# The low halves of 32 retrieval weights made early and read back from DRAM, and four gates moved

## Chip, cores and metric

The kernel runs on one core of a Trainium2 chip. The metric is the device time of one execution in microseconds (us). The engines are TensorE (PE; its weight loads are shown as PEld), VectorE (DVE), ScalarE (ACT), GpSimd (POOL) and SyncE (SP), which here does nothing but issue DMA transfers. The five run their own instruction streams in order, and an instruction that waits holds up those behind it.

## The reference

Two transformer blocks on 512 positions of width 1024, all in fp32, batch 1. The change touches the first. It computes, cut to what matters:

```python
h = modulate(rmsnorm(x, norm1_g), sh1, sc1)
q, k, v, gu, gv, ga, gb = split(h @ w_in)
y_a = neighborhood_attention(q, k, v, k_c, v_c, na_rpb)
y_b = spatial_gating(gu, gv, gm_ln_g, gm_ws, gm_bs)
x = x + g1 * (sigmoid(ga) * (y_a @ w_proj_a) + sigmoid(gb) * (y_b @ w_proj_b)) @ w_out
h2 = modulate(rmsnorm(x, norm2_g), sh2, sc2)
# peer_ffn, for each position, 8 heads:
s_top, i_top = top_k(q . sub_keys, 16)          # two halves of 128 keys
best_s, best_pos = top_k(all 16 x 16 sums, 16)  # which 16 of 16384 experts
wgt = softmax(best_s) * gelu(expert_u[experts] . h2)
x = x + g2 * sum(wgt * expert_v[experts])
```

Three of four position blocks compute the hidden values of all 16384 experts as dense products (128 weight blocks `uT[i]` of 128 experts each) and pick from them; the fourth block gathers its experts' rows.

## The kernel before

**Weights.** A product in fp32 is made of three fp32r products, hi·hi, hi·lo and lo·hi (`mm3`, L859 to L862). For each 512 KB weight block `weight` (L849 on) issues a load from SP into a `raw` buffer, ACT writes the rounded copy `hi` (L854), and DVE writes the rest, `lo` = raw - hi (L856). There are four `raw`, three `hi` and three `lo` buffers. A `raw` buffer is free when its `lo` is done. The rows `adar` of the modulation weights, which DVE accumulates through this whole stretch, take the same four buffers.

**Stages of the first block, by the trace.** Up to about 120 us the inputs, the modulation and the products `gv` and `gu`. To 176 us the second branch: gates 0 to 3 (`gate`, a product of 24 matmuls on a `win` block and a sigmoid), then a loop over eight output blocks b (12 matmuls each on half a `wpb` block), which for b of 4 to 7 computes gate b before the product. From 176 us the query, key and value products and the heads' attention, to 382 us. Then the loop over eight `wpa` half-blocks (to 404 us), the `wout` blocks (to 450 us), the retrieval's queries with their top 16 (475 to 572 us), and the retrieval proper:

```python
work = Work(*[retrieve(n) for n in range(NT - 1, -1, -1)])
while work.parts:
    spilled(first)
    work.go(RH)
    if len(work.parts) < NT:
        gat.go(GH0)
    first += 1
```

`spilled(i)` is the dense product of one `uT` block with 384 positions (24 matmuls) and a gelu (L377). Between the products the four blocks' retrieval steps go, interleaved: POOL forms the 256 sums of a head (`cand`, L306), DVE takes their top 16 (L272 to L276), DVE compares and POOL multiplies the expert indices (`eq`, L321 and L323, on POOL two in a row for each block), DVE adds them up (L329); and, for the gathered block, POOL issues indirect DMAs of 1 MB (`rows`, L178) that DVE reduces (L172, L169). After 740 us the remaining `uT` blocks go on without `retrieve`. The order of instructions on each engine is set by a scheduler when the kernel is built.

Of the kernel before, what the change touches and what calls it, by code (L numbers as in the profile page):

```python
# [8 lines left out]
F32 = mybir.dt.float32  # L9
F32R = mybir.dt.float32r  # L10
# [3 lines left out]
AF = mybir.ActivationFunctionType  # L14
# [4 lines left out]
P = 128  # L19
# [111 lines left out]
HALVES = slice(0, S // 2), slice(S // 2, S)  # L131
DT = 3
AB, LA = 3, 1
NR, TC, IG = 32, 24, 8
RH, GH0, BH, GH1, GF, GO, VP = 2.4, 1.0, 2.3, 1.2, 3.4, 4, 999


def peer(ctx, tc, I, banks, mod, mid, x1, R, vec, gain, ident, weight, mm3, proj, proj_many, split, enter):

    nc = tc.nc  # L140
    T = DT * P
    with ExitStack() as c2:
# [82 lines left out]
        with ExitStack() as c3:  # L225
# [2 lines left out]
            hl = phh.tile([P, KB, S], F32R, name="hl2")  # L228
            h = (hh, hl)
            bank = banks(mm=(4, 5, 6), S=(2, 3), T=(7, 0), h=(4, 5), o=(0, 2, 7, 3, 1, 6))  # L230
            sources, queue = [I["wq"][hp] for hp in range(NHP)] + [I["uT"][i] for i in range(P)], []

            def fill(n=3):
                while len(queue) < n and sources:
                    queue.append(weight(sources.pop(0)))

            with tc.tile_pool(name="tn", bufs=1) as tn:
                s2 = tn.tile([P, KB], F32, name="s2")
# [578 lines left out]
def body(ctx, tc, I, out):  # L817
# [32 lines left out]
    def weight(src, pool=False):  # L850
# [5 lines left out]
        (nc.gpsimd if pool else nc.vector).tensor_sub(lo, raw, hi.bitcast(F32))  # L856
        return hi, lo

    def mm3(ps, w, x, first, last):  # L859
        nc.tensor.matmul(ps, w[0], x[0], start=first, stop=False)  # L860
        nc.tensor.matmul(ps, w[0], x[1], start=False, stop=False)  # L861
        nc.tensor.matmul(ps, w[1], x[0], start=False, stop=last)  # L862
# [64 lines left out]
    with ExitStack() as c1:  # L927
# [175 lines left out]
            gate(gbm[:, n, :], 28 + n)  # L1103
            next(later, None)
        for b in range(KB):
            if b >= NT:
                gate(gbm[:, b, :], 28 + b)
            if b % 2 == 0:
                wb = weight(I["wpb"][b // 2])
            b_ps = bank("S")  # L1110
            proj(b_ps, wb, (ybh[:, 0], ybh[:, 1]), 4, (b % 2) * 4)
            nc.vector.tensor_mul(gbm[:, b, :], gbm[:, b, :], b_ps)
            next(later, None)
        c1g.close()

        sga = pz.tile([P, KB, S], F32, tag="sga", name="sga")
# [80 lines left out]
        for b in range(4):  # L1197
# [3 lines left out]
            for qb in range(4):  # L1201
                bias = bp.tile([P, 2, 256], F32, tag="bias", name="bias", bufs=2)
                nc.sync.dma_start(bias, I["bias"][qb * 4 + b])
                nc.gpsimd.tensor_add(bias, bias, mask[:, qb, :].unsqueeze(1).broadcast_to([P, 2, 256]))
                q, g = slice(qb * P, (qb + 1) * P), WIN[qb] * 64
                for j in range(2):
                    i = qb * 2 + j
                    s_ps = bank("S")
                    nc.tensor.matmul(s_ps, qs[:, j, q], window(kk, j, g), start=True, stop=False)
                    nc.tensor.matmul(s_ps, qx[:, j, q], window(kk, j, g), start=False, stop=True)  # L1210
                    nc.vector.tensor_add(s_ps[:, 0:256], s_ps[:, 0:256], bias[:, j, :])
                    nm = bp.tile([P, 1], F32, tag="nm", name="nm")
                    nc.vector.tensor_reduce(nm, s_ps, AX.X, ALU.max, negate=True)
                    pr = bp.tile([P, S], F32, tag="pr", name="pr")
                    nc.scalar.activation(pr, s_ps, AF.Exp, bias=nm, accum_out=rs[:, i:i + 1])
                    tp = bank("T")
                    for c in range(4):
                        nc.tensor.transpose(tp[:, c * P:(c + 1) * P], pr[:, c * P:(c + 1) * P], ident)
                    pT = bp.tile([P, 4, P], F32, tag="pT", name="pT")
                    if j:  # L1220
                        nc.scalar.activation(pT.rearrange("p j q -> p (j q)"), tp, AF.Copy)
                    else:
                        nc.vector.tensor_copy(pT.rearrange("p j q -> p (j q)"), tp)
                    for c in range(4):
                        v = VCH[qb][c] if c < 2 else 5 + c
                        nc.tensor.matmul(o_ps[:, i * 64:i * 64 + 64], pT[:, c, :], V9[:, v, j * 64:j * 64 + 64],
                                         start=c == 0, stop=c == 3)
                    if j and beside[b]:
                        beside[b].pop(0)()
                    next(later, None)  # L1230
            while beside[b]:
                beside[b].pop(0)()
# [18 lines left out]
        with tc.tile_pool(name="pm", bufs=1) as pm, tc.tile_pool(name="sr2", bufs=1) as sr:  # L1251
# [4 lines left out]
            for b in range(KB):  # L1256
# [4 lines left out]
                nc.vector.tensor_mul(sga[:, b, :], sga[:, b, :], a_ps)  # L1261
                nc.vector.tensor_add(sga[:, b, :], sga[:, b, :], gbm[:, b, :])
                split(mh[:, b, :], ml[:, b, :], sga[:, b, :])
            ms, held, R = bank("T"), {}, mid.tile([P, S], F32, name="nR")

            def wout(b, w, c=slice(0, S)):
# [9 lines left out]
            for b in range(KB):  # L1276
                late.append((b, weight(I["wout"][b])))
                if b < KB - 3:
                    wout(*late.pop())
            for half in HALVES:  # L1280
                for a in late:
                    wout(*a, half)
                rfactor(sr, ms[:, half], S // 2, into=R[:, half], tag="h")
    st = peer(ctx, tc, I, banks, mod, cm, x1, R, vec, gain, ident, weight, mm3, proj, proj_many, split, enter)
    second(ctx, tc, I, out, st, vec, gain, ident, ones, weight, mm3, proj, proj_many, squares, rsqrt, rfactor, split)


# [12 lines left out]
```

## Time and profile before

| | |
|---|---|
| median of 3 runs | 2567.55 us (2566.6 to 2568.09) |
| the profiled execution | 2567.01 us, its span 2565.2 us |
| mean granted clock | 0.987 |
| PE busy | 2487.4 us, 97% of the span |
| DVE, ACT, POOL busy | 70%, 42%, 12% |

The span is what the profiler records, from the first to the last instruction. Busy shares are averages over the whole span; the stages above have different limits.

### The profile page before, as it was taken

What the parts mean: (1) busy time and instruction counts of PE and PEld (TensorE: products, weight loads), DVE (VectorE), ACT (ScalarE), POOL (GpSimd) and SP (SyncE); (2) the same over time, 40 slices, a digit from 0 to 9 for tenths busy, and PEclk for the clock granted to TensorE, in tenths of its full rate; (3) what the DMA queues carried; (4) which work ended last, traced back from release to release, by engine and by line L of the source; (5) the groups of instructions that cost most, each with busy time, mean ns of one, the idle gap of its engine ahead of it and who ended that gap; (6) DMA issues with size and microseconds to landing.
All of it is one profiled execution on the core that took longest, in us unless ns stands there. A gap on an engine that the chain in (4) does not pass through costs nothing.

```text
span 2565.2 us, 34641 instructions
## 1 busy us (share of the span) xinstructions
PE 2487.4 (97%) x13153; PEld 2137.1 (83%) x13153; DVE 1795.4 (70%) x3041; ACT 1066.7 (42%) x1844; POOL 307.2 (12%) x198
## 2 busy tenths in 40 slices
PE   7999999998889999999999999998999999999998
PEld 4788888888889999999988888886788888888887
DVE  6656745899989888878888888877765334533345
ACT  6524453433344444444444433435433323422343
POOL 0001100004331111122222222200000000000000
PEclk8999999999899999999999999999999999999999
DMA  6353533325667888899998999972112233223254
GB/s 239 127 172 125 169 100 118 101 83 169 226 247 278 300 291 294 289 345 346 328 356 314 317 355 362 358 288 75 58 42 83 90 99 99 91 99 99 98 182 163
DMA packets 145814, 511.28 MB, mean 199 GB/s; under 512 B 13680, under 2 KB 39408, under 8 KB 125936
## 3 DMA queue, kind: packets, MB, share of 16 engines
q1 hardware_dynamic: 114464, 330.14, 37.7%
q0 software_dynamic: 18432, 134.23, 14.3%
q10 hardware_dynamic: 12752, 44.70, 4.6%
q8 instruction: 103, 1.69, 0.3%
q14 instruction: 63, 0.52, 0.1%
HBM read 465.50 MB, written 43.52 MB: 198 GB/s over the span
## 4 chain that ended last, share of the span: by engine, by line
PE 85%; DVE 10%; ACT 2%; issue 1%; DMA 1%; POOL 0%; DVEq 0%; SPq 0%; ACTq 0%; POOLq 0%
PE ps_mm L860 13%; PE ps_mm L862 13%; PE ps_mm L861 12%; PE ps_o L862 7%; PE ps_o L861 7%; PE ps_o L860 7%; PE ps_S L860 3%; PE ps_S L861 3%; PE ps_S L862 3%; PE ps_S L197 3%; DVE lo L856 2%; PE ps_A L861 2%; PE ps_A L862 2%; PE ps_A L860 2%; PE ps_h L862 1%
## 5 line engine op out<-in xcount | busy, mean ns | idle before, releaser
L856 DVE TENSOR_TENSOR lo<-raw,hi 128x1024 fp32r<-128x1024 f32 x473 | 586.6, 1242 | 367.1 <-ACT hi L854 357.3
L854 ACT ACTIVATE hi<-raw 128x1024 fp32r<-128x1024 f32 x474 | 500.0, 1056 | 752.3 <-PE ps_mm L861 423.8
L862 PE MATMUL ps_mm<-hh,lo 128*128 128x512 f32 (+2 forms) x1784 | 655.4, 368 | 28.9 <-DVE lo L856 28.8
L860 PE MATMUL ps_mm<-hh,hi 128*128 128x512 f32 (+2 forms) x1784 | 662.0, 372 | 7.6 <-ACT gv L1058 2.4
L861 PE MATMUL ps_mm<-hl,hi 128*128 128x512 f32 (+2 forms) x1784 | 655.5, 368 | 2.5 <-DVE hl L919 2.2
L862 PEld LDWEIGHTS ps_mm<-hh,lo 128*128 128x128 f32 x1784 | 339.5, 190 | 65.8 <-DVE lo L856 31.7
L860 PEld LDWEIGHTS ps_mm<-hh,hi 128*128 128x128 f32 x1784 | 338.6, 190 | 44.9 <-ACT gv L1058 2.9
L861 PEld LDWEIGHTS ps_mm<-hl,hi 128*128 128x128 f32 x1784 | 339.6, 190 | 38.2 <-DVE hl L919 3.3
L178 POOL DMA_INDIRECT rows<-in_uv,dix x128 | 217.4, 1699 | 747.7 <-DVE act L427 190.0
L862 PE MATMUL ps_o<-hi,wl 128*128 128x512 f32 x768 | 299.5, 390 | 0.4 <-DVE wl L919 0.4
L860 PE MATMUL ps_o<-hi,wh 128*128 128x512 f32 x768 | 298.9, 389 | 0.7 <-ACT wh L918 0.7
L861 PE MATMUL ps_o<-lo,wh 128*128 128x512 f32 x768 | 299.2, 390 | 0.0
L172 DVE SCALAR_TENSOR_TENSOR rows<-rows,hn 128x1024 f32<-128x1024 f32 x128 | 160.0, 1250 | 18.2 <-ACT act L377 8.3
L169 DVE SCALAR_TENSOR_TENSOR accn<-rows,wgt,accn 128x1024 f32<-128x1024 f32 x128 | 167.3, 1307 | 4.4 <-ACT wgt L175 2.9
L862 PEld LDWEIGHTS ps_o<-hi,wl 128*128 128x128 f32 x768 | 144.2, 188 | 31.4 <-DVE wl L919 1.4
L860 PEld LDWEIGHTS ps_o<-hi,wh 128*128 128x128 f32 x768 | 144.2, 188 | 30.4 <-ACT wh L918 1.0
L861 PEld LDWEIGHTS ps_o<-lo,wh 128*128 128x128 f32 x768 | 144.2, 188 | 29.4
L918 ACT ACTIVATE wh<-act 128x384 fp32r<-128x384 f32 x104 | 54.7, 526 | 236.8 <-PE ps_o L861 217.3
L193 DVE TENSOR_TENSOR gi<-oh,gt 128x1536 bf16<-128x1536 bf16 x96 | 91.4, 955 | 0.9
L191 DVE TENSOR_TENSOR oh<-iob,ji 128x1024 bf16<-128x1024 bf16 x96 | 65.9, 689 | 26.8 <-PE ps_S L197 26.2
L197 PE MATMUL ps_S<-gi,oh 128*128 128x128 bf16 x1152 | 78.1, 219 | 0.0
L861 PE MATMUL ps_S<-hl,hi 128*128 128x512 f32 x200 | 78.0, 390 | 0.0
(396 smaller groups left out, 3621.0 us busy)
## 6 DMA issues: line engine op xcount, KB each, us to landing
raw<-in_uT SPq DMA_DIRECT2D x128, 512.0 KB
raw<-in_uv SPq DMA_DIRECT2D x128, 512.0 KB
raw<-in_win SPq DMA_DIRECT2D x82, 512.0 KB
raw<-in_wd SPq DMA_DIRECT2D x44, 512.0 KB
act<-act ACTq DMA_DIRECT2D x52, 384.0 KB
act<-act SPq DMA_DIRECT2D x52, 384.0 KB
gs<-stage ACTq DMA_DIRECT2D x16, 1152.0 KB
ring<-gs SPq DMA_DIRECT2D x12, 1536.0 KB
```

What stands on the lines that cost most here:

```text
L169: nc.vector.scalar_tensor_tensor(accn, rows.pop(k - 3)[:, D:], wgt[:, c], accn, op0=ALU.mult, op1=ALU.add)
L172: paced(nc.vector.scalar_tensor_tensor(r[:, :D], r[:, :D], 1.0, hn, op0=ALU.mult, op1=ALU.mult, accum_out=dot[:, c]))
L178: paced(nc.gpsimd.indirect_dma_start(out=r, out_offset=None, in_=I["uv"], in_offset=bass.IndirectOffsetOnAxis(ap=dix[:, k:k + 1], axis=0)))
L191: nc.vector.tensor_tensor(oh, io, each(ji[:, t0 // 4], 2), ALU.is_equal)
L193: nc.vector.tensor_tensor(gi, oh[:, 1].unsqueeze(1).broadcast_to([P, 3, 2, P, 2]), each(gt[:, t0 // 4], 3), ALU.mult)
L197: nc.tensor.matmul(g_ps[:, t, :], oh[:, 0, t // 2, :, t % 2], gi[:, j, t // 2, :, t % 2], start=j == 0, stop=j == 2)
L854: nc.scalar.activation(hi, raw, AF.Copy)
L856: (nc.gpsimd if pool else nc.vector).tensor_sub(lo, raw, hi.bitcast(F32))
L860: nc.tensor.matmul(ps, w[0], x[0], start=first, stop=False)
L861: nc.tensor.matmul(ps, w[0], x[1], start=False, stop=False)
L862: nc.tensor.matmul(ps, w[1], x[0], start=False, stop=last)
L918: nc.scalar.activation(hi, src, AF.Copy)
```

## The change

A generator `ahead` handles the blocks `uT[4]` to `uT[35]`, 32 in all, one at each step: SP loads the block into a `raw` buffer, ACT makes `hi`, DVE writes raw - hi back into `raw`, and POOL issues a DMA that stores it into `lows` in DRAM. It is stepped eight times in the loop over the second branch's output products, 12 times in the attention, eight times in the `wpa` loop and four times in the `wout` loop. In the retrieval, `weight_kept` loads these blocks as before and makes `hi` as before, but gets `lo` by a DMA from `lows` that POOL issues; DVE does nothing for it. The other 96 blocks go through `weight`. In the second branch gates 4 and 5 are computed ahead of the first output product, gate 6 ahead of the third and gate 7 ahead of the fourth. Two lines are added to `peer` and 26 to `body` ahead of the code in question, so `weight`'s `lo` is L858 after, the early subtraction L870, the store L871 and the load of `lo` L884.

```diff
+            sources = [lambda i=i: weight(I["wq"][i]) for i in range(NHP)] + [lambda i=i: weight_kept(i) for i in range(P)]
...
+    lows = ctx.enter_context(tc.tile_pool(name="da", bufs=1, space=bass.MemoryType.DRAM)).tile([AN, P, D], F32, name="lows")
+
+    def ahead():
+        for i in range(AN):
+            raw = wp.tile([P, D], F32, tag="raw", name="raw", bufs=4)
+            nc.sync.dma_start(raw, I["uT"][A0 + i])
+            hi = wp.tile([P, D], F32R, tag="hi", name="hi", bufs=3)
+            nc.scalar.activation(hi, raw, AF.Copy)
+            nc.vector.tensor_sub(raw, raw, hi.bitcast(F32))
+            nc.gpsimd.dma_start(lows[i], raw)
+            yield
+
+    ahead = ahead()
+
+    def weight_kept(i):
+        if not A0 <= i < A0 + AN:
+            return weight(I["uT"][i])
+        raw = wp.tile([P, D], F32, tag="raw", name="raw", bufs=4)
+        nc.sync.dma_start(raw, I["uT"][i])
+        hi = wp.tile([P, D], F32R, tag="hi", name="hi", bufs=3)
+        nc.scalar.activation(hi, raw, AF.Copy)
+        lo = wp.tile([P, D], F32R, tag="lo", name="lo", bufs=3)
+        nc.gpsimd.dma_start(lo, lows[i - A0])
+        return hi, lo
...
         for b in range(KB):
-            if b >= NT:
-                gate(gbm[:, b, :], 28 + b)
+            for g in (4, 5) if b == 0 else (b + 4,) if b in (2, 3) else ():
+                gate(gbm[:, g, :], 28 + g)
             if b % 2 == 0:
                 wb = weight(I["wpb"][b // 2])
...
             next(later, None)
+            next(ahead, None)
...
                     if j and beside[b]:
                         beside[b].pop(0)()
+                    if not j and qb != 1:
+                        next(ahead, None)
                     next(later, None)
...
                 split(mh[:, b, :], ml[:, b, :], sga[:, b, :])
+                next(ahead, None)
...
                 if b < KB - 3:
                     wout(*late.pop())
+                    next(ahead, None)
+            for _ in ahead:
+                pass
```

The queue of SP in the second branch's output loop, before (`raw` from `win` is a gate's weight, from `wpb` an output weight, and `adar` the modulation's rows):

```order
L1027 DMA adar_1047<-in_adaB 128x1024
L852 DMA raw_1050<-in_wpb 128x1024
L1027 DMA adar_1070<-in_adaB 128x1024
L1027 DMA adar_1087<-in_adaB 128x1024
L852 DMA raw_1090<-in_wpb 128x1024
L1027 DMA adar_1110<-in_adaB 128x1024
L1027 DMA adar_1127<-in_adaB 128x1024
L852 DMA raw_1141<-in_win 128x1024
L852 DMA raw_1172<-in_wpb 128x1024
L1027 DMA adar_1192<-in_adaB 128x1024
```

The same place in the changed kernel, from gate 4 on (`raw` from `uT` is a unit of `ahead`):

```order
L854 DMA raw_1054<-in_win 128x1024
L854 DMA raw_1086<-in_win 128x1024
L854 DMA raw_1117<-in_wpb 128x1024
L1055 DMA adar_1137<-in_adaB 128x1024
L867 DMA raw_1140<-in_uT 128x1024
L1055 DMA adar_1160<-in_adaB 128x1024
L867 DMA raw_1163<-in_uT 128x1024
L854 DMA raw_1170<-in_win 128x1024
L854 DMA raw_1201<-in_wpb 128x1024
L1055 DMA adar_1221<-in_adaB 128x1024
L867 DMA raw_1224<-in_uT 128x1024
L854 DMA raw_1231<-in_win 128x1024
```

Two gates' weights now stand ahead of the first output weight, and a unit of `ahead` stands between every two output blocks, ahead of gate 6 (`raw_1170`), which gets the buffer of the first unit (`raw_1140`) once this is stored.

The queue of POOL in the retrieval around the first pair of `eq`, before:

```order
L306 TENSOR_TENSOR cand_5274<-top_4057 128x256
L306 TENSOR_TENSOR cand_5452<-top_4057 128x256
L306 TENSOR_TENSOR cand_5495<-top_4057 128x256
L323 TENSOR_TENSOR eq_5319<-eq_5319,tif_5049 128x8x16x16
L323 TENSOR_TENSOR eq_5326<-eq_5326,tif_5049 128x8x16x16
L306 TENSOR_TENSOR cand_5536<-top_4057 128x256
L306 TENSOR_TENSOR cand_5544<-top_4057 128x256
L306 TENSOR_TENSOR cand_5587<-top_4057 128x256
```

The same place in the changed kernel:

```order
L884 DMA lo_5465<-lows_86 128x1024
L308 TENSOR_TENSOR cand_5647<-top_4252 128x256
L308 TENSOR_TENSOR cand_5690<-top_4252 128x256
L884 DMA lo_5507<-lows_86 128x1024
L325 TENSOR_TENSOR eq_5514<-eq_5514,tif_5244 128x8x16x16
L325 TENSOR_TENSOR eq_5521<-eq_5521,tif_5244 128x8x16x16
L884 DMA lo_5553<-lows_86 128x1024
L308 TENSOR_TENSOR cand_5731<-top_4252 128x256
L308 TENSOR_TENSOR cand_5739<-top_4252 128x256
L884 DMA lo_5592<-lows_86 128x1024
```

The loads of `lo` now stand in POOL's queue between the `cand` and `eq`, here one just ahead of the pair of `eq` and the next just behind it. The third pair of `eq` stands unbroken too, with a gather and then a load of `lo` behind it:

```order
L884 DMA lo_6114<-lows_86 128x1024
L325 TENSOR_TENSOR eq_6388<-eq_6388,tif_6067 128x8x16x16
L325 TENSOR_TENSOR eq_6395<-eq_6395,tif_6067 128x8x16x16
L179 DMA rows_6083<-in_uv,dix_3915 128x2048
L884 DMA lo_6156<-lows_86 128x1024
```

In the second and the fourth pair a load of `lo` stands between the two `eq`.

## Rows read from the trace of the kernel before

**Rows 1.** Page, parts 1 and 5: the engines, the groups of hi and lo.

```profile
PE 2487.4 (97%) x13153; PEld 2137.1 (83%) x13153; DVE 1795.4 (70%) x3041; ACT 1066.7 (42%) x1844; POOL 307.2 (12%) x198
...
L856 DVE TENSOR_TENSOR lo<-raw,hi 128x1024 fp32r<-128x1024 f32 x473 | 586.6, 1242 | 367.1 <-ACT hi L854 357.3
L854 ACT ACTIVATE hi<-raw 128x1024 fp32r<-128x1024 f32 x474 | 500.0, 1056 | 752.3 <-PE ps_mm L861 423.8
```

**Rows 2.** Windows by stage: engines' busy us, granted clock, DMA share, GB/s.

```profile
120.00:176.00 56.00, 51.92 (x236) 41.71 (x235) 30.05 (x34) 13.90 (x17) 0.00 (x0) 0.94 0.50 160
185.00:382.00 197.00, 194.46 (x1168) 167.84 (x1167) 123.04 (x175) 98.58 (x167) 21.25 (x15) 1.00 0.39 126
382.00:404.00 22.00, 22.00 (x98) 18.05 (x97) 18.05 (x25) 8.68 (x13) 0.00 (x0) 1.00 0.43 153
572.00:740.00 168.00, 141.71 (x781) 140.00 (x781) 165.07 (x401) 64.51 (x105) 73.56 (x48) 0.93 0.55 188
```

**Rows 3.** Groups in 572 to 740 us: busy us, mean ns | idle before.

```profile
L862 PE MATMUL ps_mm<-hh,lo 128*128 128x384 f32 x258 | 89.4, 347 | 26.3 <-DVE lo L856 26.2
...
L856 DVE TENSOR_TENSOR lo<-raw,hi 128x1024 fp32r<-128x1024 f32 x32 | 44.5, 1392 | 0.0
...
L323 POOL TENSOR_TENSOR eq<-eq,tif 128x2048 bf16<-128x2048 bf16 x8 | 33.9, 4257 | 13.0 <-DVE eq L321 13.0
L306 POOL TENSOR_TENSOR cand<-top 128x256 f32<-128x256 f32 x30 | 22.6, 755 | 156.0 <-DVE rest L273 83.3 <-DVE bx L275 72.7
L178 POOL DMA_INDIRECT rows<-in_uv,dix x10 | 17.0, 1704 | 3.6 <-ACT act L377 2.2 <-issue 0.5
```

**Rows 4.** Waits in 572 to 740 us: total us, times, longest us.

```profile
POOL cand L306 <- DVE bx L275: 72.7, 28, 8.4
...
PE ps_mm L862 <- DVE lo L856: 26.2, 4, 9.2
```

**Rows 5.** Windows of 10 us, columns as in Rows 2.

```profile
630.00:640.00 10.00, 7.83 (x46) 7.51 (x44) 10.00 (x9) 4.11 (x6) 9.05 (x3) 1.00 0.44 159
640.00:650.00 10.00, 7.76 (x30) 7.76 (x31) 10.00 (x25) 3.30 (x7) 3.41 (x3) 0.66 0.67 246
```

**Rows 6.** Timeline of POOL, 570 to 745 us: start, us, what [idle before].

```profile
632.84 8.26 POOL L323 TENSOR_TENSOR eq<-eq,tif 128x2048 bf16<-128x2048 bf16 x2 [0.93 <-DVE eq L321]
...
720.16 2.99 POOL L178 DMA_INDIRECT rows<-in_uv,dix  x1 [2.21 <-ACT act L377]
```

**Rows 7.** Timeline of DVE in 628 to 652 us.

```profile
633.81 3.78 DVE L335 TENSOR_TENSOR ex<-bs 128x128 f32<-128x128 f32 x1
637.51 4.67 DVE L856 TENSOR_TENSOR lo<-raw,hi 128x1024 fp32r<-128x1024 f32 x1
```

**Rows 8.** Timeline of ACT in 618 to 630 us, first and last of three.

```profile
620.71 1.06 ACT L854 ACTIVATE hi<-raw 128x1024 fp32r<-128x1024 f32 x1 [2.72 <-PE ps_mm L861]
...
629.03 1.06 ACT L854 ACTIVATE hi<-raw 128x1024 fp32r<-128x1024 f32 x1 [2.72 <-PE ps_mm L861]
```

**Rows 9.** The tile rows in 570 to 760 us: its gathers on POOL.

```profile
L178 POOL DMA_INDIRECT rows<-in_uv,dix x12: 958/1760/2991, 620.5 to 754.9; - x12
...
DMA to landing us min/median/max: 5.8/7.4/9.4
```

**Rows 10.** Timeline of SP's queue in 118 to 182 us.

```profile
122.19 0.33 SPq L852 DMA_DIRECT2D raw<-in_wpb  x1
```

**Rows 11.** Timeline of ACT in 118 to 182 us.

```profile
125.49 1.06 ACT L854 ACTIVATE hi<-raw 128x1024 fp32r<-128x1024 f32 x1 [1.70 <-DMA raw<-in_wpb]
126.45 0.61 ACT L918 ACTIVATE yb<-ybt 128x512 fp32r<-128x512 f32 x1
```

**Rows 12.** Timeline of PE, 118 to 182 us; 12 matmuls from 117.67 to 120.16.

```profile
117.67 0.39 PE L860 MATMUL ps_mm<-hh,hi 128*128 128x512 f32 x1
...
120.16 0.39 PE L862 MATMUL ps_mm<-hh,lo 128*128 128x512 f32 x1
...
127.12 1.22 PE L860 MATMUL ps_S<-yb,hi 128*128 128x512 f32 x2 [3.96 <-ACT yb L918]
```

More of the change, by code (lines that the diff above doesn't have):

```diff
@@ L133, with peer @@
 AB, LA = 3, 1
+A0, AN = 4, 32
 NR, TC, IG = 32, 24, 8
 RH, GH0, BH, GH1, GF, GO, VP = 2.4, 1.0, 2.3, 1.2, 3.4, 4, 999
-def peer(ctx, tc, I, banks, mod, mid, x1, R, vec, gain, ident, weight, mm3, proj, proj_many, split, enter):
+def peer(ctx, tc, I, banks, mod, mid, x1, R, vec, gain, ident, weight, weight_kept, mm3, proj, proj_many, split, enter):
     nc = tc.nc
@@ L230, in peer @@
             bank = banks(mm=(4, 5, 6), S=(2, 3), T=(7, 0), h=(4, 5), o=(0, 2, 7, 3, 1, 6))
-            sources, queue = [I["wq"][hp] for hp in range(NHP)] + [I["uT"][i] for i in range(P)], []
+            sources = [lambda i=i: weight(I["wq"][i]) for i in range(NHP)] + [lambda i=i: weight_kept(i) for i in range(P)]
+            queue = []
             def fill(n=3):
                 while len(queue) < n and sources:
-                    queue.append(weight(sources.pop(0)))
+                    queue.append(sources.pop(0)())
             with tc.tile_pool(name="tn", bufs=1) as tn:
@@ L1283, in body @@
                 rfactor(sr, ms[:, half], S // 2, into=R[:, half], tag="h")
-    st = peer(ctx, tc, I, banks, mod, cm, x1, R, vec, gain, ident, weight, mm3, proj, proj_many, split, enter)
+    st = peer(ctx, tc, I, banks, mod, cm, x1, R, vec, gain, ident, weight, weight_kept, mm3, proj, proj_many, split, enter)
     second(ctx, tc, I, out, st, vec, gain, ident, ones, weight, mm3, proj, proj_many, squares, rsqrt, rfactor, split)
```

## The prediction

> **What bounds the kernel now.** The page comes first: PE is busy for 97% of the span and DVE for 70% [rows 1], so on the average the matmuls are the limit, and work taken from DVE is worth something only where PE waits for DVE. The windows by stage show where that is [rows 2]. In the attention PE works 194.46 of 197 us and in the `wpa` loop 22.00 of 22: nothing is to be had there. In the second branch, 120 to 176 us, it works 51.92 of 56. In the retrieval, 572 to 740 us, it works 141.71 of 168 while DVE works 165.07: here DVE is the bound. The waits of this stage say with what: PE idles 26.2 us in four pieces, the longest 9.2, and each ends with a `lo` of DVE [rows 4].
>
> How such a piece comes about is seen at 633 us. POOL starts its pair of `eq`, 8.26 us [rows 6]. On DVE the next two instructions, a small subtraction and a `lo`, take 3.78 and 4.67 us [rows 7], where a `lo` has a mean of 1.242 over the whole span [rows 1]: each ends about when an `eq` ends. PE, without its `lo`, idles, and after that its granted clock, 1.00 from 630 to 640 us, is 0.66 from 640 to 650 [rows 5], so that it spent part of those 10 us on the lower of its two levels, 1.2 instead of 2.4 GHz. An idle piece is thus paid for twice.
>
> What the stage would take with PE never waiting: its third matmuls number 258, eight to a product, so 32.25 products [rows 3]; undisturbed, three `hi` start from 620.71 to 629.03, each at the pace of a product, so 4.16 us a product [rows 8]. 32.25 x 4.16 = 134 us. Of the 168, 34 are lost: 26.3 idle [rows 3] and 7.7 at the lower clock, or 0.3 for each us idle. No more than 34 can be won by this change in this stage.
>
> **The change, part by part.**
>
> *Retrieval: DVE's `lo` removed.* 32 x 1.392 = 44.5 us go from DVE [rows 3]; it keeps some 120 of 165, less than PE's 134. In its place POOL issues 32 loads in order with its other work. The trace has no plain DMA from POOL. The nearest rows: a 1 MB gather from POOL occupies it 0.96 to 2.99 us, median 1.76, and lands 5.8 to 9.4 us after issue, median 7.4 [rows 9]; a 512 KB load from SP, issued at 122.19, lets its `hi` start at 125.49, 3.30 us later [rows 10, 11]. The bounds for a 512 KB transfer from POOL are 3.3 and 9.4; I take 5, halfway between the 3.3 and the median gather with its double size, rounded down. For the issue I take the gather's mean, 1.7 [rows 3]. POOL's own work becomes 33.9 for `eq`, 22.6 for `cand`, 17.0 for gathers and 32 x 1.7 = 54 for the loads [rows 3]: 128 us. That is below 134, but not by much.
>
> What replaces the wait: `lo` has three buffers, so the next load can go out only when PE has done with the product three earlier, and it can stand behind a pair of `eq`. When a pair begins, PE has at most the product it is in and two more: on average 2.5 x 4.16 = 10.4 us of cover. At the first pair the next load is issued behind both `eq` (8.26 us) and lands 5 later, 13.26 us: 2.9 uncovered. At the third a gather of 1.7 stands between too: 4.6. In the second and fourth pairs a load stands between the `eq`: 4.2 + 1.7 + 5 = 10.9, about nothing. Besides, POOL waits for DVE ahead of its `cand`, 72.7 us in 28 waits, up to 8.4 [rows 4], and a load behind such a `cand` is late when the wait falls badly; I allow 1 us in each of the four blocks, 4 in all. Together 11.5 us idle, with the lower clock 11.5 x 1.3 = 15 of the 34. **Gain 19**; bounds 34 (all covered) and 0 (landing 9.4, which makes the four pieces 7.3, 4.9, 8.9 and 4.9 us: the 26 of now).
>
> *Second branch.* Gone is PE's wait of 3.96 us at 123 us [rows 12]: ACT's `yb` at 126.45 stood behind a `hi` that waited for a `wpb` block to land [rows 11], and gates 4 and 5 now cover both. With the lower clock behind it (granted 0.94 in this stage) about 4 x 1.8 = 7 us, since 56 - 51.92 leaves 4 and the clock's 6% of 51.92 another 3. Added are eight units. Each holds a `raw` buffer for load 3.3, `hi` 1.06, subtraction 1.24 and store 5, 10.6 us; an ordinary weight holds one for 5.6, an `adar` about 4.5 (the load and one DVE instruction of a `lo`'s size). Eight units, eight weights (four gates, four `wpb`) and eight `adar` need 85 + 45 + 36 = 166 buffer-us, over four buffers 41.5 us. PE has for the same loop 4 gates x 24 and 8 blocks x 12 matmuls at 0.227 us (12 from 117.67 to 120.16 [rows 12]), 43.6 us. So the buffers are as full as PE is, and in a fixed order chains stand out. Gate 6 takes the first unit's buffer: 10.6 + 5.6 = 16.2 from that unit's issue, against gates 4, 5 and two blocks, 16.3. The last `wpb` stands behind an `adar` that waits for the fourth store: 16 against a gate and three blocks, 13.6. The query weight stands behind two units that wait for the fifth and sixth store: about 17.5 against four blocks, 10.9, and the stall just had. That is 0 + 2.4 + 4.2, and some five places where a `hi` (1.06) or an accumulation on DVE is ahead of what is wanted, 1 us each: 12 added, 7 removed. **Cost 5**; bounds 0 (transfer 3.3) and 12 (9.4, or more of it with the lower clock).
>
> *Attention.* 12 subtractions, 15 us of DVE, and 12 `hi`, 13 us of ACT; DVE is free 74 of 197 us and ACT 98 [rows 2]. That time covers them, except where PE waits for a softmax step that stands behind such an instruction. PE is idle 2.5 us here now, so the engines run well ahead of it. **Cost 2**; bounds 0 and 8 (about a third of the 28 us in front of PE).
>
> *`wpa` and `wout` loops.* Eight units and four weights need 8 x 10.6 + 4 x 5.6 = 107 buffer-us, over four buffers 27, where PE needs 22.0 [rows 2]; in `wout` the buffers suffice. Some loads go out ahead of the loop. **Cost 4**; bounds 0 and 10.
>
> Sum: -19 + 5 + 2 + 4 = -8. From the profiled execution, 2567.01 us (span 2565.2 and 1.8 around it; the median of the runs is 0.5 higher), **2559 us**.
>
> The Trainium skill, page "DMA: Bandwidth & Descriptors", section "Anatomy of one DMA — SWDGE (gpsimd) path", has such a transfer take 2.0 us and its bytes by 436 GB/s, an estimate of 3.2 us for 512 KB. By it the first and third pairs would leave 1.1 and 2.8, the gain would be about 24, the early work would cost about 5, and the time would be about 2548. For the 1 MB gathers the same formula gives 4.4 us, and the trace has 5.8 to 9.4 [rows 9], so here it runs low and I keep 5.
>
> **The rivals.**
>
> *Full gain.* The loads land in 3.3 us and the early work hides: -34 to -26, 2533 to 2541. For it: PE stands still only in four pieces, and DVE drops below PE. Against it: the loads stand behind `eq` and `cand`, and POOL has 128 us of work in a stage of 134.
>
> *POOL becomes the bound.* If a load holds POOL 2.99 us, the longest issue at 720.16 [rows 6], the 32 take 96 and POOL has 170 us of work, the 168 of now and a little more. The retrieval gains nothing, the early work costs 11: 2578. It decides from an issue of about 1.9 us, where POOL's work reaches PE's 134. For it: POOL also waits for DVE 72.7 us of the stage, and what it waits is not in its 128. Against it: the median issue is 1.76 [rows 9]. The Trainium skill names a cause: by the page "SBUF — State Buffer", section "Who interferes with whom", a transfer from POOL is starved while DVE holds the ports that both share. The pair of `eq` with DVE's 3.78 and 4.67 us [rows 7] agrees that the two block each other, in the other direction.
>
> *The stores hold the buffers.* A store of 9.4 us makes a unit hold its buffer for 15: second branch 8 x 15 + 81 = 201 over 4, 50 us against 43.6, `wpa` loop 36 against 22. With the lower clock behind the stalls that is +12, +10 and in the attention +8, while the loads of `lo`, no stores, keep 15 of gain: +15, 2582. It decides from a store of about 7 us, where the costs reach the gain of 19.
>
> **How the numbers follow.** The forecast's case, 2550 to 2568, has 0.47; full gain 0.20; POOL as the bound 0.19; held buffers 0.14. About 0.2%, 5.1 us, is what a measurement here can tell from no change: below 2562.4 is faster, above 2572.7 slower. The first case is faster with 0.35 and the same with 0.12; full gain is faster; the third is slower with 0.16 and the same with 0.03; the fourth slower with 0.10 and the same with 0.04. Faster 0.55, same 0.19, slower 0.26. The range 2540 to 2580 leaves out most of full gain's better half and the worse ends of the last two, 0.2 in all.
>
> **What would show it.** Right: in the retrieval DVE's `lo` x32 gone, the stage at about 149 us, PE's idle time near 11 us, ended by the DMA of `lo` and mostly behind the first and third pair of `eq`; the query product some 5 us later than the 176 us of now; PE waits in the `wpa` loop that are not there now. Wrong: POOL busy throughout the retrieval; issue rows over 2 us; PE idle as long as before; stores that land after 7 us or more; or softmax steps in the attention that PE waits for.

## Result, and the profile after

The changed kernel takes 2601.07 us (median of 4 runs, 2594.52 to 2605.57) against 2567.82 of the kernel before (2566.6 to 2569.33): 1.0123 times as long, 95% interval 1.011 to 1.0136. It is slower by about 32 us, where 8 us faster were forecast. The profiled execution has a span of 2600.1 us, 34.9 more than before.

The page of the changed kernel, its line of engines and the group of the third matmuls, says first that PE works almost as long but waits for something new:

```profile
PE 2505.5 (96%) x13153; PEld 2141.7 (82%) x13153; DVE 1789.7 (69%) x3041; ACT 1100.4 (42%) x1876; POOL 334.9 (13%) x262
...
L890 PE MATMUL ps_mm<-hh,lo 128*128 128x512 f32 (+2 forms) x1784 | 657.9, 369 | 24.3 <-DMA lo<-lows 19.7
```

For 19.7 us a `lo` from DRAM ends PE's idle time where a `lo` of DVE did before (26.2, [rows 4]). The rest is in the stages ahead. Five groups, from the views of single tiles, mark the stages by their first and last start: the query copies (`qf`), the context's products (`hc`, the last one near the end of the attention's products), the `wout` products (`mh`), the gelus behind the `uT` products, and the matmuls behind the retrieval that build its dense weights (called the build here). Before:

```profile
L1136 ACT ACTIVATE qf<-ps_mm x4: 580/599/600, 181.9 to 301.4; 128x512 f32<-128x512 f32 x4
...
L860 PE MATMUL ps_mm<-hc,hi x64: 277/283/366, 186.4 to 328.3; 128*128 128x256 f32 x64
...
L860 PE MATMUL ps_mm<-mh,hi x88: 278/283/469, 403.8 to 449.3; 128*128 128x256 f32 x48, 128*128 128x512 f32 x40
...
L377 ACT ACTIVATE act<-ps_mm x104: 464/470/495, 574.6 to 1109.3; 128x384 f32<-128x384 f32 x104
...
L197 PE MATMUL ps_S<-gi,oh x1152: 217/218/238, 770.5 to 1091.5; 128*128 128x128 bf16 x192
```

And after:

```profile
L1165 ACT ACTIVATE qf<-ps_mm x4: 583/600/600, 194.5 to 327.1; 128x512 f32<-128x512 f32 x4
...
L888 PE MATMUL ps_mm<-hc,hi x64: 277/283/366, 196.9 to 354.5; 128*128 128x256 f32 x64
...
L888 PE MATMUL ps_mm<-mh,hi x88: 277/283/499, 439.0 to 486.2; 128*128 128x256 f32 x48, 128*128 128x512 f32 x40
...
L379 ACT ACTIVATE act<-ps_mm x104: 467/472/495, 612.7 to 1142.4; 128x384 f32<-128x384 f32 x104
...
L198 PE MATMUL ps_S<-gi,oh x1152: 217/218/238, 803.6 to 1124.7; 128*128 128x128 bf16 x192
```

First `qf` 181.9 to 194.5: 12.6 us lost in the second branch. Last `hc` 328.3 to 354.5: 26.2 lost by then, 13.6 of them in the attention. First gelu 574.6 to 612.7: 38.1, another 11.9 in `wpa`, `wout` and the queries, 9.0 of them ahead of the first `wout` product (403.8 to 439.0). First matmul of the build 770.5 to 803.6: 33.1. So the early work costs 38 us, and the retrieval, from the first gelu to the build, has gone from 195.9 to 190.9 us: a gain of 5, where up to 34 were lost to PE's waits and the lower clock. Not all of the 38 is waiting: in the windows between these marks, from 120 us on, PE is idle 35.5 us instead of 12.2, and its matmuls take 15 us longer, at a granted clock of 0.93, 0.97 and 0.97 instead of 0.94, 1.00 and 0.99.

**The early stages.** The waits of SP's queue in the changed kernel, 120 to 440 us (total, times, longest):

```profile
SPq L867 <- DMA lows<-raw: 41.2, 10, 13.9
...
SPq L854 <- DMA lows<-raw: 27.5, 8, 7.6
...
SPq L1055 <- DMA lows<-raw: 18.6, 6, 5.2
```

SP stands 87 us before buffers that a store still holds, and behind it stand the loads of weights. That sum is not yet a cost: in the kernel before, SP stood 88.0 us before buffers that a weight's `lo` held (120 to 410 us), and PE's waits from 120 to 440 us came to some 6 us. It counts where a load that PE needs goes out too late. One case, on SP, ACT and PE (timelines):

```profile
171.83 0.33 SPq L1055 DMA_DIRECT2D adar<-in_adaB  x1
177.54 0.33 SPq L867 DMA_DIRECT2D raw<-in_uT  x1
177.97 0.37 SPq L854 DMA_DIRECT2D raw<-in_win  x1
```

```profile
181.23 1.06 ACT L869 ACTIVATE hi<-raw 128x1024 fp32r<-128x1024 f32 x1 [3.38 <-DMA raw<-in_uT]
182.52 1.06 ACT L856 ACTIVATE hi<-raw 128x1024 fp32r<-128x1024 f32 x1 [0.24 <-DMA raw<-in_win]
```

```profile
183.63 0.80 PE L888 MATMUL ps_mm<-hh,hi 128*128 128x512 f32 x1 [5.71 <-ACT hi L856]
```

SP's load of the eighth unit at 177.54 had to wait 5.4 us for a store; the query's weight (`win`) is issued behind it at 177.97. On ACT the `hi` of a unit whose block has just landed goes first, at 181.23, and the query's `hi` is made at 182.52, as soon as its own block is there (ACT waits 0.24 us more for it): here SP's order makes PE late, and ACT's adds next to nothing. PE waits 5.71 us, and the 10 us around the end of this wait show a granted clock of 0.66 (windows, columns as in rows 2):

```profile
180.00:190.00 10.00, 6.33 (x18) 4.61 (x19) 4.55 (x4) 3.17 (x3) 0.53 (x1) 0.66 0.94 339
```

That ACT waits for units at all is new. Between 120 and 200 us alone, from the waits of that stretch:

```profile
ACT hi L869 <- DMA raw<-in_uT: 27.6, 7, 6.3
```

**The retrieval.** The windows of the whole stage and of two pieces of it, the groups, PE's wait, and the landing times of the loads (`lo`) and stores (`lows`):

```profile
608.00:803.00 195.00, 175.30 (x959) 171.85 (x958) 148.90 (x410) 77.81 (x129) 88.53 (x83) 0.95 0.85 301
660.00:670.00 10.00, 1.60 (x11) 1.28 (x9) 7.95 (x13) 2.04 (x4) 9.36 (x7) 0.79 0.90 305
670.00:680.00 10.00, 10.00 (x41) 10.00 (x42) 4.52 (x17) 1.44 (x2) 1.78 (x3) 0.70 0.76 284
```

```profile
L325 POOL TENSOR_TENSOR eq<-eq,tif 128x2048 bf16<-128x2048 bf16 x8 | 33.8, 4238 | 4.8 <-DVE eq L323 4.8
...
L308 POOL TENSOR_TENSOR cand<-top 128x256 f32<-128x256 f32 x30 | 19.1, 644 | 108.5 <-DVE rest L275 84.4 <-DVE bx L277 23.4 <-DVE bx L278 0.6
...
L884 POOL DMA_DIRECT2D lo<-lows x32 | 18.3, 571 | 39.4 <-PE ps_mm L890 37.5 <-PE ps_T L351 1.9
...
L858 DVE TENSOR_TENSOR lo<-raw,hi 128x1024 fp32r<-128x1024 f32 x8 | 9.8, 1220 | 9.5 <-ACT hi L856 9.5
```

```profile
PE ps_mm L890 <- DMA lo<-lows: 19.7, 8, 8.4
```

```profile
L884 POOL DMA_DIRECT2D lo<-lows x32: 540/570/656, 615.2 to 774.3; - x32
...
DMA to landing us min/median/max: 3.5/7.0/10.3
```

```profile
DMA to landing us min/median/max: 2.9/4.0/7.2
```

DVE has 8 `lo` left, POOL's issue of a load takes 0.57 us, and a load lands 3.5 to 10.3 us after it. PE's longest wait, 8.4 us, lies at the second pair of `eq`; POOL's timeline there, and PE's, with the waits at the first and third pair beside it:

```profile
653.56 0.56 POOL L884 DMA_DIRECT2D lo<-lows  x1
...
657.37 4.61 POOL L325 TENSOR_TENSOR eq<-eq,tif 128x2048 bf16<-128x2048 bf16 x1 [1.91 <-DVE eq L323]
661.93 0.60 POOL L884 DMA_DIRECT2D lo<-lows  x1
662.84 1.02 POOL L179 DMA_INDIRECT rows<-in_uv,dix  x1 [0.31 <-ACT act L379]
663.85 0.60 POOL L884 DMA_DIRECT2D lo<-lows  x1
664.44 3.70 POOL L325 TENSOR_TENSOR eq<-eq,tif 128x2048 bf16<-128x2048 bf16 x1
```

```profile
641.74 0.54 PE L890 MATMUL ps_mm<-hh,lo 128*128 128x384 f32 x1 [1.77 <-DMA lo<-lows]
...
661.25 0.34 PE L889 MATMUL ps_mm<-hl,hi 128*128 128x384 f32 x1
669.99 0.69 PE L890 MATMUL ps_mm<-hh,lo 128*128 128x384 f32 x1 [8.40 <-DMA lo<-lows]
...
714.76 0.69 PE L890 MATMUL ps_mm<-hh,lo 128*128 128x384 f32 x1 [3.27 <-DMA lo<-lows]
```

Between the loads at 653.56 and 661.93 stand a `cand` and an `eq` that waits for DVE and then takes 4.61 us. PE runs out at 661.6, 4.2 us after the `eq` began, so it had no three products of cover; the load lands some 8 us later, with a 1 MB gather and another load issued behind it. At the first pair, which begins at 629.99, PE ran until 639.97 and waited 1.77 us.

### The profile page after: what moved, and what is told of

Its sections match the earlier page's. It is cut to its first block, busy times and chain, and to the rows that moved or that the text cites. A ratio compares the mean times of both kernels' runs of the same rounds, so it can differ in the third digit from the quotient of the medians.

```text
span 2600.1 us, 34864 instructions
## 1 busy us (share of the span) xinstructions
PE 2505.5 (96%) x13153; PEld 2141.7 (82%) x13153; DVE 1789.7 (69%) x3041; ACT 1100.4 (42%) x1876; POOL 334.9 (13%) x262
## 4 chain that ended last, share of the span: by engine, by line
PE 81%; DVE 8%; DMA 5%; ACT 2%; issue 2%; POOL 1%; SPq 0%; DVEq 0%; ACTq 0%; POOLq 0%
PE ps_mm L888 12%; PE ps_mm L890 12%; PE ps_mm L889 12%; PE ps_o L890 7%; PE ps_o L889 7%; PE ps_o L888 7%; PE ps_S L888 3%; PE ps_S L890 3%; PE ps_S L889 3%; PE ps_S L198 3%; PE ps_A L889 2%; PE ps_A L890 2%; PE ps_A L888 1%; DMA raw<-in_uT 1%; PE ps_h L890 1%
## 5 line engine op out<-in xcount | busy, mean ns | idle before, releaser
L858 DVE TENSOR_TENSOR lo<-raw,hi 128x1024 fp32r<-128x1024 f32 x441 | 541.3, 1229 | 364.3 <-ACT hi L856 357.0
L856 ACT ACTIVATE hi<-raw 128x1024 fp32r<-128x1024 f32 x442 | 466.1, 1056 | 668.9 <-PE ps_mm L889 360.5
L890 PE MATMUL ps_mm<-hh,lo 128*128 128x512 f32 (+2 forms) x1784 | 657.9, 369 | 24.3 <-DMA lo<-lows 19.7
L179 POOL DMA_INDIRECT rows<-in_uv,dix x128 | 211.6, 1653 | 753.5 <-DVE act L429 195.9
L192 DVE TENSOR_TENSOR oh<-iob,ji 128x1024 bf16<-128x1024 bf16 x96 | 65.8, 688 | 26.8 <-PE ps_S L198 26.2
```

The lines of the kernel that those rows point to most:

```text
L179: paced(nc.gpsimd.indirect_dma_start(out=r, out_offset=None, in_=I["uv"], in_offset=bass.IndirectOffsetOnAxis(ap=dix[:, k:k + 1], axis=0)))
L192: nc.vector.tensor_tensor(oh, io, each(ji[:, t0 // 4], 2), ALU.is_equal)
L856: nc.scalar.activation(hi, raw, AF.Copy)
```

## The experiments

Times are medians, ratios are to the kernel before, with their 95% intervals; 0.1% is 2.6 us. The kernel without gathers was run once. A stage's time comes from one profiled execution: from the first gelu to the build it is 195.9 to 196.7 us in the traces of all kernels with `eq` on POOL and every `lo` by DVE.

**The gates alone.** Edit, in the kernel before:

```diff
-            if b >= NT:
-                gate(gbm[:, b, :], 28 + b)
+            for g in (4, 5) if b == 0 else (b + 4,) if b in (2, 3) else ():
+                gate(gbm[:, g, :], 28 + g)
```

> The kernel before with only the four gates moved; no early units, low halves by DVE. Theory A (the move does what the prediction said of it): the 4 us wait of PE at 123 us and the low clock behind it go, 7 us gained: about 2561. Rival B (the wait goes elsewhere, to the next output weight): within 2 us of before, about 2568.

Measured: 2563.82 us, 0.9975 (0.9965 to 0.9985), 6 us faster. The prediction's 7 us for this part hold: `qf` starts at 175.9 instead of 181.9, and the wait for `yb` is gone from PE with none in its place in the second branch. In its trace 4.0 of the 6 us are left at the last `hc` and 3.0 at the build.

**The early units alone.**

```diff
-[lambda i=i: weight_kept(i) for i in range(P)]
+[lambda i=i: weight(I["uT"][i]) for i in range(P)]
```

> The changed kernel, but the retrieval makes all low halves on DVE as before; the 32 stored low halves are written and never read. The traces put the early work at +38 us by the start of the retrieval and the gain there at 5. If the two parts are independent: 2568 + 38 = about 2606. Rival (the early work only looks dear because later waits would have absorbed it): under 2590.

Measured: 2612.54, 1.0164 (1.0133 to 1.0196), 42 us slower with the gates' gain in it. The early work is as dear by itself; the rival falls.

**The early units without their stores.** early_alone with:

```diff
             nc.vector.tensor_sub(raw, raw, hi.bitcast(F32))
-            nc.gpsimd.dma_start(lows[i], raw)
```

> As early_alone, but the early units are not stored: load, high half and subtraction stay, the raw buffer is free when DVE is done. Theory A (the cost is that a raw buffer is held until its store has landed, 4 to 7 us more, and the loads behind it on SP wait): the cost falls from 38 to 10 us or less, 2578 or less. Rival B (the cost is the 32 high halves and subtractions that stand ahead of what PE waits for on ACT and DVE, and the 16 MB of loads): at least 25 us remain, 2593 or more.

Measured: 2593.5, 1.0088 (1.0067 to 1.0108). The stores make about 19 us of the cost, and some 23, or 29 with the gates' gain given back, remain. By its number the rival B holds, just (2593 or more); but the store is a large part too, so both count.

**The reading alone.** No units, gates as before, and in `weight_kept` the weight block itself is read, so that the low half is left out of the product and only its transfer stays:

```diff
-        nc.gpsimd.dma_start(lo, lows[i - A0])
+        nc.gpsimd.dma_start(lo, I["uT"][i].bitcast(F32R))
```

> The kernel before (gates not moved, no early units), but in the retrieval POOL loads 512 KB into the low buffer of 32 blocks where DVE made it; what is loaded is the weight block itself, so the low half is left out of the result's meaning, with the same bytes and the same place in the queues. If the gain seen there (5 us) is the retrieval's own: about 2563. If it was cut short by the early work: 19 us or more, 2549 or less.

Measured: 2562.44, 0.9964 (0.9951 to 0.9977), 9 us by the ratio; the stage takes 192.9 us in its trace instead of 195.9. The early work did not cut the gain short: the retrieval itself gains little by reading. How much differs from trace to trace: with all 32 read and `eq` on POOL the stage takes from 186.8 (after_adar) to 192.9 us.

**A high buffer for the units.** The changed kernel with one buffer more, outside the weights' three (the line that opens its pool is left out here and below):

```diff
-            hi = wp.tile([P, D], F32R, tag="hi", name="hi", bufs=3)
+            hi = own[0].tile([P, D], F32R, tag="ehi", name="ehi", bufs=1)
```

> The changed kernel, but the early units write their high half into a buffer of their own, outside the three that the products' weights use; raw buffers and stores as in the changed kernel. Theory A (a unit between two weights also takes one of three high buffers, which come free only when PE has used them, so that ACT, which works in order, stands before a unit's high half and the next weight's behind it): at least 8 us of the 2601 go, 2593 or less. Rival B (what holds is that the unit's load lands late on ACT's order and in SP's queue, whatever the buffer): 2598 or more.

Measured: 2595.77, 1.0105 (1.0088 to 1.0121), some 5 us better than the changed kernel, with intervals that overlap. It lies between the two theories. In its trace the first gelu starts at 611.2, only 1.5 us earlier, and the rest lies in the retrieval (187.4 us): the high buffers are a small part of the early cost, if any.

**A raw buffer for the units, loaded by POOL.**

```diff
-            raw = wp.tile([P, D], F32, tag="raw", name="raw", bufs=4)
-            nc.sync.dma_start(raw, I["uT"][A0 + i])
+            raw = own[0].tile([P, D], F32, tag="early", name="early", bufs=1)
+            nc.gpsimd.dma_start(raw, I["uT"][A0 + i])
```

> The changed kernel, but the early units' raw block is one buffer of its own, loaded and stored from POOL's queue, so that neither SP nor the four raw buffers see the early units; the high half stays in the shared three. Theory A (raw buffers and SP's order are the larger part of the early cost, 19 of 43 us by the store and more by the loads): 2580 or less, so at least 20 us better than the changed kernel. Rival B (one buffer makes the units so slow that ACT and DVE, in order, wait for them): 2601 or more.

Measured: 2677.3, 1.0423 (1.0405 to 1.044), 76 us slower than the changed kernel. With a single buffer a unit's load goes out only after the store ahead has landed. Its waits, 120 to 500 us:

```profile
ACT hi L871 <- DMA early<-in_uT: 82.6, 14, 11.7
...
PE ps_S L890 <- ACT hi L856: 37.9, 6, 12.2
```

ACT stands 82.6 us before units' loads, up to 11.7 at a time, and PE's output products stand behind weights' `hi` that are next on ACT. It doesn't test the raw buffers, as it was meant to, but it shows what ACT's order costs when units land late.

**Reading without the gathers between.** read_alone with:

```diff
                 work.go(RH)
-                if len(work.parts) < NT:
-                    gat.go(GH0)
```

> As read_alone, but no gathers between the retrieval's products; they all come after it, so the total time says little. Looked at: PE's idle time by low loads in the retrieval, about 20 us in the changed kernel, and how long the loads take to land (median 7.0). Theory A (the loads are late because the gathers, 1 MB each, share the DMA engines with them): landing 4 us or less, idle 8 us or less. Rival B (they are issued late, behind the sums and the pairs of index products on POOL): idle 12 us or more although they land fast.

PE's idle time by loads and their landing in read_alone, 560 to 790 and 560 to 760 us, and then the same here:

```profile
PE ps_mm L876 <- DMA lo<-in_uT: 23.5, 9, 8.0
```

```profile
DMA to landing us min/median/max: 3.7/6.4/11.7
```

```profile
PE ps_mm L874 <- DMA lo<-in_uT: 17.6, 6, 4.1
```

```profile
DMA to landing us min/median/max: 3.6/4.8/8.8
```

Landing falls from a median of 6.4 to 4.8 us, idle time only from 23.5 to 17.6. Both are above theory A's numbers: the gathers delay the loads, but most of the waiting stays.

**Index products on DVE.** gates_alone with one word changed:

```diff
-                    nc.gpsimd.tensor_tensor(e4, e4, tif[:, :, j, :]...
+                    nc.vector.tensor_tensor(e4, e4, tif[:, :, j, :]...
```

> The kernel before with the gates moved, and the eight index products (eq) of the retrieval on DVE instead of POOL; no early units. Theory A (PE's four idle pieces in the retrieval come of the pairs of eq on POOL, during which DVE's instructions take 4 to 5 us instead of 0.3 to 1.2): with DVE paying 8 times 1.2 to 2.1 us but no longer stretched, the pieces shrink to half, 2564 of gates_alone falls to 2550 or less. Rival B (DVE is simply full, 165 of 168 us): 2564 or more.

Measured: 2547.34, 0.9922 (0.9905 to 0.9938), 20 us faster than before and 14 (by the ratios) to 16 (by the medians) faster than gates_alone. DVE's timeline at the first pair:

```profile
592.25 4.48 DVE L323 TENSOR_TENSOR eq<-eq,tif 128x2048 bf16<-128x2048 bf16 x2
596.65 1.21 DVE L856 TENSOR_TENSOR lo<-raw,hi 128x1024 fp32r<-128x1024 f32 x1
```

The two products take 4.48 us on DVE, and the `lo` behind them its usual 1.21, where it took 4.67 in the shadow of POOL's pair [rows 7]. The stage takes 183.4 us. DVE is as full as before (window of the retrieval):

```profile
560.00:760.00 200.00, 185.93 (x1066) 180.78 (x1065) 195.50 (x479) 84.05 (x145) 41.95 (x44) 0.97 0.64 218
```

It has taken eight products more into a stage 13 us shorter than in gates_alone (196.6 us). So a part of what had filled it was being held up.

**Units without a high half.** early_nostore with

```diff
-            hi = wp.tile([P, D], F32R, tag="hi", name="hi", bufs=3)
-            nc.scalar.activation(hi, raw, AF.Copy)
-            nc.vector.tensor_sub(raw, raw, hi.bitcast(F32))
+            nc.vector.tensor_sub(raw, raw, raw)
```

> As early_nostore (2593.5), but a unit has no high half either: its block is loaded into one of the four raw buffers and one subtraction on DVE frees it; nothing of it is used. So the 32 loads, the four raw buffers and 15 MB stay, and ACT does nothing for the units. Theory A (what is left without the stores is ACT: a unit's high half waits there for the unit's load, and the next weight's high half, of which PE has need, stands behind it): 2575 or less. Rival B (it is the raw buffers and SP's order): 2585 or more.

Measured: 2578.46, 1.0043 (1.0026 to 1.006). Without `hi` the cost falls by 12 us (15 by the medians); 17 over gates_alone (15) stay for the loads, their buffers and the subtraction. The median lies between the two theories.

**Twelve units, in the attention only.** `A0, AN = 4, 12`, and the three other calls of `next(ahead, None)` and the loop that empties `ahead` left out.

> The changed kernel with 12 units instead of 32, all of them in the attention, none in the second branch, the output projections and after; the retrieval reads low halves for blocks 4 to 15 and makes the others on DVE. Theory A (the cost lies where PE's own products follow each other in 3 to 5 us, in the second branch and the output projections; in the attention there is room): attention costs 5 or less, the retrieval gains 3, against gates_alone at 2564 no more than 2567. Rival B (each unit costs about 1.2 us wherever it stands): 2564 + 14 - 3, 2573 or more.

Measured: 2575.12, 1.003 (1.0017 to 1.0042). Rival B holds: 11 to 14 us over gates_alone. In its trace the attention, from the first `qf` (174.3) to the last `hc` (337.2), takes 162.9 us, where gates_alone takes 148.4: 14.5 for 12 units. The retrieval takes 189.7 us there, 7 less; but this execution, 2570.39 us, is the fastest of six, so that gain is not to be set against the median. PE's waits in its attention, 185 to 345 us:

```profile
PE ps_T L1246 <- ACT pr L1243: 4.0, 5, 2.1
...
PE ps_mm L888 <- DVE kk L1186: 3.3, 1, 3.3
```

These are a softmax step and a key's high half that ACT and DVE finish late. In gates_alone PE waits there 2.0 us, all for `pr`. The waits alone are not the 14.5: the granted clock from the first `qf` to the last `hc` is 0.96 instead of 0.99.

**The changed kernel with the index products on DVE.** Edit as in eq_dve.

> The changed kernel with the eight index products of the retrieval on DVE, so that no pair of eq stands ahead of the loads of low halves on POOL. Theory A (the retrieval gained 5 instead of 19 because the loads stand behind eq): PE's idle time by low loads falls from 20 us to 8 or less, and the total by 10 or more, 2591 or less. Rival B (it is the transfers, two of 512 KB a product and the gathers, 0.69 to 1.07 of the DMA engines): idle 15 us or more, 2596 or more.

Measured: 2587.32, 1.0079 (1.0062 to 1.0096), 11 to 14 us better than the changed kernel. PE's waits for loads in the stage, and landing:

```profile
PE ps_mm L890 <- DMA lo<-lows: 7.1, 4, 3.9
```

```profile
DMA to landing us min/median/max: 4.3/6.6/12.2
```

Idle 7.1 instead of 19.7 although the loads land hardly sooner (median 6.6 instead of 7.0). So PE's waits came of late issue, behind `eq`, more than of the transfer. The stage takes 171.7 us in this trace, 19 less than in the changed kernel and 12 less than in eq_dve: with `eq` out of POOL's queue, reading the low halves is worth more than twice the 5 us of before.

**One index product of a pair on DVE.** `(nc.vector if j else nc.gpsimd).tensor_tensor(...)` in eq_dve.

> As eq_dve (2547), but only the second of each pair of index products on DVE, the first on POOL. If what counts is the length of a pair in which DVE's instructions are held up: one eq holds DVE for 4 us instead of 8, and DVE has 4 x 2.3 us less to do than in eq_dve: 2543 to 2547. If any eq on POOL is worse than 2.3 us more on DVE: 2550 or more.

Measured: 2549.96, 0.993 (0.9914 to 0.9947): not told apart from eq_dve; moving only one of the two is no better.

**The modulation's rows out of the shared buffers**, in early_noact, in the changed kernel and in gates_alone:

```diff
-                    raw = wp.tile([P, D], F32, tag="raw", name="adar", bufs=4)
+                    raw = own.tile([P, D], F32, tag="adar", name="adar", bufs=1)
```

> As early_noact (2578.5, where the loads of the units alone cost 14.6 over gates_alone), but the modulation's rows (adar) go through one buffer of their own instead of the four raw buffers; their place in SP's queue stays. Theory A (the raw buffers: units, weights and adar together need 41 of 44 us of four buffers in the second branch): with adar's 9 us gone the cost halves at least, 2571 or less. Rival B (SP's order: each load waits behind the one ahead, whatever its buffer): 2576 or more.

> The changed kernel with adar in one buffer of its own. Theory A (raw buffers held until a store has landed): 2590 or less. Rival B (SP's order and ACT's): 2597 or more.

> The control: gates_alone (2564) with adar in one buffer of its own, no units. PE waits for no load in the second branch there, so nothing is to be won: 2562 to 2566. If one buffer for adar is itself a hindrance: 2568 or more.

Measured: 2573.95 (1.0023, 1.0013 to 1.0034), 2579.21 (1.0046, 1.0029 to 1.0063) and 2564.68 (0.9989, 0.9979 to 0.9999). The control gains nothing. The changed kernel loses 20 of its 32 us of slowdown, as theory A has it. The loads' cost over their control falls from 17 to 9 us by the ratios, but noact_adar lies between its two theories, and in the traces its first gelu starts only 2.0 us earlier than in early_noact (581.9 and 583.9). By the trace of after_adar the first gelu starts at 588.9, 23.8 us earlier than in the changed kernel, of 41.8 that lie between that and gates_alone (570.9); this execution is the fastest of four. So about half of the early cost goes with `adar` out of the shared buffers. SP stands before stores there as long as in the changed kernel (120 to 440 us):

```profile
SPq L854 <- DMA lows<-raw: 43.0, 14, 6.6
SPq L867 <- DMA lows<-raw: 41.1, 10, 13.8
```

84 us against 87: how long SP waits is by itself not the cost. In the traces the weights and the units keep their order in SP's queue, but several rows of `adar` have moved in it, against what was expected, so the buffers and the places of `adar` in the queue are not told apart.

A rival without a run of its own is the added traffic. The `win` blocks land 3.9 us after issue (median, 120 to 440 us) against 4.3 in gates_alone, which gives no sign of it; the four `wpa` blocks take 7.2.

## Why the prediction was wrong, step by step

**What bounds the kernel: right.** PE's four idle pieces in the retrieval and their cause, the pair of `eq` with DVE held up behind it, hold; eq_dve, which only moves the pair, gains 14 to 16 us. DVE was the bound there in part because it was held up: with the pair on it, it is as full in a stage 13 us shorter.

**The gates: right**, 7 forecast, 6 measured.

**The early units: the step that failed.** "So the buffers are as full as PE is" was counted as a rate, 41.5 us of four buffers against 43.6 of PE, and its cost put at 12 in the second branch, with 2 in the attention and 4 in the `wpa` and `wout` loops. They cost 12.6 + 6 for the gates' gain that hides in it, about 19, then 13.6 and 11.9. The landing time of a store was not at fault: 5 us was taken, and the median is 4.0, the longest 7.2. So the rival "the stores hold the buffers" did not get its condition, a store of about 7 us, and yet the kernel became slower than the 2582 of that rival; stores of 4 us already make 19 us of the cost. Two things stand in the place of the rate. A ring of buffers as full as PE, used in a fixed order, is not enough: taking only `adar` out of it gives 20 us back (after_adar). That it has no slack and passes on every lateness is the likely reason and was not shown by itself. And a unit isn't carried out in the background: its `hi` waits on ACT, in order, for its own load (27.6 us from 120 to 200 us, where no such wait was before; 82.6 in own_raw_pool), and the weight's `hi` that PE needs stands behind (PE's output products wait 37.9 us for it in own_raw_pool). The lower clock behind the new waits, which the prediction left to its bounds, is in these costs too. By what was left out, the loads and the subtraction come to some 17 us, the high halves 12, the stores 19; the intervals of the runs are 5 to 16 us wide, so the split is rough, and loads and subtraction weren't separated.

**The attention: wrong by the cover.** "DVE is free 74 of 197 us and ACT 98. That time covers them" is no cover where the order is fixed: 12 units cost 1.2 us each in the trace of early_att12, where 2 in all were forecast, by 4.0 us of waits for a softmax step, 3.3 for a key's half and the lower clock among other things.

**The retrieval: direction right, size wrong.** Forecast 19, measured 5 (9 by itself). Of its terms the issue, 1.7, was 0.57, so that POOL, 88.5 of 195 us busy, never came near a bound and that rival falls. The uncovered time was taken as 11.5 us and is 19.7; with 19.7 the prediction's own sum, 34 - 1.3 x 19.7, gives a gain of 8. The term that was wrong is the second pair, put at about nothing and in fact the longest piece, 8.4 us. The first and the third came out near their terms (1.77 us against 2.9, 3.27 against 4.6), and at the first the cover was the 10 us that were taken. At the second it was 4.2: "on average 2.5 x 4.16 = 10.4 us of cover" takes PE to be three products behind the loads at each pair, but up to 664 us no load in POOL's timeline waits for one of the three `lo` buffers, that is, POOL, not PE, is the later one. And the landing, taken as 5 from loads in stages that moved 160 and 188 GB/s [rows 2], is 7.0 in one that moves 301: with two blocks for each product and the gathers between, the stage's DMA share is 0.85. Without the gathers it is 4.8 (read_nogather); without the `eq` in front PE idles only 7.1 us (after_eqdve). Both act; the place in POOL's queue acts more.

The estimate of 3.2 us by the Trainium skill, page "DMA: Bandwidth & Descriptors", section "Anatomy of one DMA — SWDGE (gpsimd) path", is about the shortest that these transfers took, 2.9 for a store and 3.5 for a load; their medians are 4.0 and 7.0. By that page the prediction's sum would have been 2548, farther off still. The page "SBUF — State Buffer", section "Who interferes with whom", says that of DVE and POOL, where both want the ports they share, the second to start waits until the first is done; the trace agrees (4.67 us for a `lo` next to `eq` on POOL, 1.21 next to `eq` on DVE), and moving the pair away was worth 14 to 16 us here.

**What would show it.** The marks that I named as wrong were there: PE idle 19.7 us where it was 26.2, and softmax steps in the attention that PE waits for. Those for long issues, for POOL busy throughout and, but for the longest, 7.2 us, for stores of 7 us or more weren't, although the kernel is slower.

## What to carry to other kernels

Work put into a stage "because its engines are half idle" is not free where every engine runs in order: ask of each added instruction what it waits for, and what of the critical stage stands behind it on that engine and that queue; and count a shared ring of buffers as full well before its sum reaches the bound. Where an engine is full, look whether its instructions are long or merely held up: moving the work that holds them up gained some 14 us with one word, where taking 44 us off the full engine gained 9 by itself and, with the work that this put elsewhere, lost 32.

## What the runs showed that was not expected

POOL's issue of a plain 512 KB DMA takes 0.57 us in the median (0.54 for a store), a third of an indirect gather's. An `eq` of 2048 elements took 4.26 us on POOL [rows 3] and 2.28 on DVE. And twelve low halves read back gained about as much in the retrieval of one trace (189.7 us against 196.6 in gates_alone) as 32 did in others (190.9 in the changed kernel, 186.8 to 192.9 in all).
